# Output projection weights split ahead of time on GpSimd and parked in HBM

## The chip, the core and the metric

The kernel runs on one core of a Trainium2 chip. The metric is the device time of one execution in microseconds (us); the time before is the median of three runs, 1128.26 us (1127.38 to 1130.19). Engines are named as in the profile: PE is TensorE (matmuls), DVE is VectorE, ACT is ScalarE, POOL is GpSimd, SP is SyncE, which issues every DMA of this kernel from one queue, in order.

## The reference, cut to what matters

One layer on 1024 tokens of width 1024. The input projection feeds a pooling group and a gated DeltaNet group; their outputs are joined into `mix`, which goes through the output projection `w_out` (1024 x 1024), and a squared-ReLU MLP follows.

```python
u = rms_norm(h, norm_mix[l])
proj = u @ w_in[l]
pool_out = pool_mixer(proj[..., :P], w_pool[l], pool_scale[l])
qkv = causal_conv_silu(proj[..., P:P + 3 * G], conv_w[l])
...
mix = jnp.concatenate([pool_out, gdn_out], axis=-1)
h = h + mix @ w_out[l]
u = rms_norm(h, norm_mlp[l])
h = h + jnp.square(jax.nn.relu(u @ w_up[l])) @ w_down[l]
return rms_norm(h, norm_final)
```

## The kernel before

Every large product is made of three matmuls in the reduced type fp32r. Each operand is split into a high part (a cast to fp32r, on ACT) and a low part (the operand less its high part, a subtraction), and the product is high x high + high x low + low x high. `split_w` (L128 to L137) does this for a weight: a DMA brings 256 KB into a tile `raw`, ACT casts it into `wh` (L135), and an engine that the caller names subtracts (L136).

The 1024 tokens are taken in two halves of 512. The input projection (`project`, L477) runs for the first half over the columns k, q, v, z, p and then for the second half over k, q, v, p, z. Each letter is two blocks of 256 columns; a block is 48 matmuls of 512 columns on PE and reads four pairs of weight tiles, which live in two rings of five buffers (`wh` and `wl`). In the first half the weights are split and both parts are stored to HBM (`keep_parts`); in the second half `load_parts` (L224) brings the parts back with two DMAs of 256 KB for each pair, so that nothing is split there.

Between these dense matmuls PE runs the chunks of the gated DeltaNet as "strands": generators that are stepped by a clock of the program's own. The order of PE is written out by this clock, and no scheduler moves it. ACT, DVE, POOL and SP are put in order by a scheduler, which estimates when operands arrive. Each engine then runs its list strictly in order, so an instruction that waits holds up all that stand behind it. The strands need ACT and DVE within a few microseconds (`invert` L611: products `pt`, `ptt`, casts `t` and `tt` on ACT at L634 and L635, masks `xx` on DVE at L628; `scan` L672: `y` on ACT at L686). The gate values of the second half (`gates`, L357) are made on ACT and DVE at L366 to L410, two loads of activation tables among them.

After the z columns of the second half comes the output projection (`out_proj2` L813, `out_proj` L803). `wout_weights(n, ks)` (L784) makes the weights of output column half n for the eight row groups k: it loads 256 KB of `w_out` into `raw` (ring of three), casts on ACT and subtracts on DVE. The groups k below 4 go into the `wh`/`wl` rings, k from 4 on into `woh`/`wol`, four buffers each, in the room that the input projection's operands `u` give up at its end (`close(upc)`, L869). For n = 0 both parts are also stored to HBM (`wdo`, L872), because tokens 512 to 1023 need them again later (L929). Tokens 0 to 511 are projected for n = 0 and n = 1, two tiles of 128 tokens at a time; the last chunks of the DeltaNet run in between as strands. The up projection follows and takes its first weights through the same `raw` ring (L1017).

## Time and profile before

| | |
|---|---|
| median of the runs | 1128.26 us |
| the profiled execution, its own time | 1130.39 us |
| its span, first to last instruction | 1128.2 us |
| TensorE clock granted, mean | 0.993 |
| first half of the input projection and its loads | about 0 to 171 us |
| second half of the input projection | about 171 to 365 us |
| output projection, both token halves | about 365 to 485 us |
| HBM read and written | 133.77 MB and 58.72 MB |

Lines of the profile read like this. A group has line, engine, operation, output<-input, how often (x), and the shortest, median and longest duration in ns with the first and last start in us; in the list of waits the columns are who waited for whom, the total in us, how many times, and the longest. A line of the timeline has start and duration in us, engine, line and operation, and in brackets the idle time of the engine just before it and what released it. `SPq` is the issue of a DMA on SP; "to landing" is the time from this issue to the arrival of its last byte.

### The profile page before, as it was taken

Reading aid. Unit: us, or ns where it says so; the run is one execution under the profiler, and the core shown is the slowest. Engines: PE = TensorE matmul, PEld = TensorE weight load, DVE = VectorE, ACT = ScalarE, POOL = GpSimd, SP = SyncE. Lnnn points to the kernel's source line nnn. Section 1 sums busy time; section 2 is a strip of 40 time slices with the busy share of each in tenths; the row PEclk is TensorE's granted clock in tenths of the full one; section 3 lists DMA queues with packets and bytes.
Section 4 is the critical chain, followed back from the end, with each engine's and each line's share of the span. In section 5 each row is a group of like instructions: output and inputs, shape, how many; then the busy total and the mean of one; then the engine's idle time right before and its main releaser. Section 6 shows DMA issues by size and latency. Waiting matters only on the chain.

```text
span 1128.2 us, 15738 instructions
## 1 busy us (share of the span) xinstructions
PE 1091.0 (97%) x5638; PEld 891.5 (79%) x5638; DVE 726.2 (64%) x1212; ACT 573.5 (51%) x1063; POOL 221.6 (20%) x217
## 2 busy tenths in 40 slices
PE   8999999999999999997899999999999999999997
PEld 6787778778888788885678888888888878888886
DVE  5787587757676864556665656565555786476584
ACT  6577566465555553555445545454543333334363
POOL 6122032020220310156333222222000000000020
PEclk9999999999999999998999999999999999999999
DMA  7877643233435620410644444444597995355662
GB/s 241 290 259 263 197 136 98 87 105 115 142 118 195 200 83 31 139 59 12 231 150 149 159 150 159 149 145 163 186 369 252 325 350 186 112 187 192 199 206 75
DMA packets 109975, 193.51 MB, mean 172 GB/s; under 512 B 10373, under 2 KB 39114, under 8 KB 109898
## 3 DMA queue, kind: packets, MB, share of 16 engines
q1 hardware_dynamic: 109898, 192.52, 50.1%
q8 instruction: 44, 0.72, 0.3%
q14 instruction: 33, 0.27, 0.1%
HBM read 133.77 MB, written 58.72 MB: 171 GB/s over the span
## 4 chain that ended last, share of the span: by engine, by line
PE 77%; ACT 4%; DVE 3%; DMA 2%; POOL 2%; issue 1%; POOLq 0%; SPq 0%; DVEq 0%; ACTq 0%
PE bank L44 55%; PE acc L44 21%; DMA x<-hd 1%; PE bank L48 1%; DVE cy L429 1%; DMA raw<-in_w_out_dram 1%; DMA wu<-in_w_up_dram 1%; POOL r L993 0%; POOL wl L1006 0%; ACT rl L554 0%; ACT wh L1005 0%; POOL rk L155 0%; POOL wu L1032 0%; DVE h L1236 0%; DVE xx L628 0%
## 5 line engine op out<-in xcount | busy, mean ns | idle before, releaser
L44 PE MATMUL bank<-th,wh 128*128 128x512 f32 x448 | 177.2, 396 | 9.9 <-DVE u L1090 6.1
L44 PE MATMUL bank<-th,wl 128*128 128x512 f32 x448 | 176.9, 395 | 2.7 <-DVE wl L1006 1.4
L44 PE MATMUL bank<-tl,wh 128*128 128x512 f32 x448 | 176.4, 394 | 0.0
L44 PE MATMUL acc<-uh,wh 128*128 128x512 f32 x320 | 129.5, 405 | 5.7 <-ACT cy L427 2.3
L44 PE MATMUL bank<-th,sh 128*128 128x512 f32 x344 | 133.8, 389 | 0.0
L44 PE MATMUL bank<-th,sl 128*128 128x512 f32 x344 | 133.8, 389 | 0.0
L44 PE MATMUL bank<-tl,sh 128*128 128x512 f32 x344 | 133.8, 389 | 0.0
L1005 ACT CAST wh<-wu 128x512 fp32r<-128x512 f32 x110 | 67.4, 620 | 122.2 <-PE bank L44 100.8
L44 PE MATMUL acc<-ul,wh 128*128 128x512 f32 x320 | 129.4, 404 | 0.0
L44 PE MATMUL acc<-uh,wl 128*128 128x512 f32 x320 | 128.7, 402 | 0.0
L1005 ACT CAST sh<-x 128x1024 fp32r<-128x1024 f32 x55 | 57.9, 1053 | 137.2 <-PE bank L44 137.1
L1006 DVE TENSOR_TENSOR sl<-x,sh 128x1024 fp32r<-128x1024 f32 x55 | 67.2, 1222 | 70.1 <-ACT sh L1005 70.1
L44 PEld LDWEIGHTS bank<-th,wh 128*128 128x128 f32 x448 | 85.0, 190 | 30.9 <-issue 7.0
L44 PEld LDWEIGHTS bank<-th,wl 128*128 128x128 f32 x448 | 84.9, 189 | 22.8 <-DVE wl L1006 2.3
L44 PEld LDWEIGHTS bank<-tl,wh 128*128 128x128 f32 x448 | 85.1, 190 | 18.4
L1006 DVE TENSOR_TENSOR wl<-wu,wh 128x512 fp32r<-128x512 f32 x98 | 74.5, 764 | 34.6 <-ACT wh L1005 33.9
L44 PEld LDWEIGHTS acc<-uh,wh 128*128 128x128 f32 x320 | 60.5, 189 | 19.2 <-ACT cy L427 4.2
L44 PEld LDWEIGHTS bank<-th,sl 128*128 128x128 f32 x344 | 64.6, 188 | 13.6
L44 PEld LDWEIGHTS bank<-th,sh 128*128 128x128 f32 x344 | 64.6, 188 | 13.4
L44 PEld LDWEIGHTS bank<-tl,sh 128*128 128x128 f32 x344 | 64.5, 188 | 13.3
L155 POOL TENSOR_TENSOR stf<-stf,mhalf 128x1 f32<-128x1 f32 x8 | 7.9, 997 | 321.3 <-DVE stf L1255 321.3
L44 PEld LDWEIGHTS acc<-uh,wl 128*128 128x128 f32 x320 | 60.6, 189 | 11.0 <-POOL wl L136 0.3
(321 smaller groups left out, 2191.6 us busy)
## 6 DMA issues: line engine op xcount, KB each, us to landing
w<-in_w_down_dram SPq DMA_DIRECT2D x55, 512.0 KB, 5.5
x<-hd SPq DMA_DIRECT2D x55, 512.0 KB, 3.3
wu<-in_w_up_dram SPq DMA_DIRECT2D x16, 1024.0 KB, 6.0
hd<-s SPq DMA_DIRECT2D x48, 256.0 KB, 2.0
raw<-in_w_in_dram SPq DMA_DIRECT2D x40, 256.0 KB, 4.1
w<-in_w_down_dram SPq DMA_DIRECT2D x32, 256.0 KB, 6.9
xin<-in_x_dram SPq DMA_DIRECT2D x8, 512.0 KB, 5.5
raw<-in_w_out_dram SPq DMA_DIRECT2D x16, 256.0 KB, 4.1
```

The lines of the kernel that those rows point to most:

```text
L44: T0.matmul(out, lhsT, rhs, start=start, stop=stop, skip_group_check=goes_on)
L48: T0.transpose(out, in_, identity)
L155: last["rsqrt"] = G.tensor_tensor(s, s, mhalf[:, :n], op=ALU.pow)
L429: V.scalar_tensor_tensor(cy, cr[:, e:e + HALF], tap[e], cy, op0=ALU.mult, op1=ALU.add)
L1005: A.copy(hi, src)
L1006: eng.tensor_tensor(lo, src, hi.bitcast(F32), op=ALU.subtract)
```

## The change

`wout_weights` no longer splits. All sixteen pieces of `w_out` (n = 0 and 1, k = 0 to 7; piece 0 to 7 and 8 to 15 below) are split by a new function, `split_wout`, which is called at three places in the second half of the input projection. Each piece takes all three buffers of the ring `raw`: the loaded weight, its high part (ACT), its low part (POOL). Both parts are stored to HBM. `wout_weights` then loads both parts with two DMAs for each piece into the same tiles that it filled before. The stores of n = 0 at the start of the output projection are gone, since all parts are in HBM.

```diff
-    def load_parts(kept, pool=None):
+    def load_parts(kept, pool=None, tags=("wh", "wl"), bufs=5):
...
-        return [split_w(wov[:, k, n * HALF:(n + 1) * HALF], [P, HALF], V,
-                        *((pools["wo"], "woh", "wol", 4) if k >= 4 else ())) for k in ks]
+        return [load_parts(wo_parts[n, k], *((pools["wo"], ("woh", "wol"), 4) if k >= 4 else ())) for k in ks]
+
+    def split_wout(n, ks):
+
+        for k in ks:
+            raw, hi, lo = (ws.tile([P, HALF], dt, name="raw", tag="raw", bufs=3) for dt in (F32, F32R, F32R))
+            nc.sync.dma_start(out=raw, in_=wov[:, k, n * HALF:(n + 1) * HALF])
+            A.copy(hi, raw)
+            G.tensor_tensor(lo, raw, hi.bitcast(F32), op=ALU.subtract)
+            wo_parts[n, k] = keep_parts(f"wdo{n}{k}", [(hi, lo)])[0]
...
         yield from project(1, "q", G)
+        split_wout(0, range(KT))
         yield from project(1, "v", G)
+        split_wout(1, range(4))
         yield from project(1, "p", G)
+        split_wout(1, range(4, KT))
         yield from project(1, "z", G, conv_done)
...
-        wo_parts.extend(keep_parts("wdo", wt[0]))
```

The order of PE is the same in both kernels. On the other engines the scheduler puts the new work earlier than the calls stand in the code: the first piece is loaded where the first `w_out` load stood before, and the last is stored among the loads of the second half's first v block.

The first place is the queue of SP around the second block of the q columns (`wd768_` are its weights). Before, only these loads stand there:

```order
L228 DMA wh_3032<-wd768_0h_737 128x512
L228 DMA wl_3034<-wd768_0l_738 128x512
L228 DMA wh_3036<-wd768_1h_741 128x512
L228 DMA wl_3038<-wd768_1l_742 128x512
L228 DMA wh_3040<-wd768_2h_745 128x512
```

In the change, the stores of piece 10 (`wdo120`), pieces 11 and 12 (`wdo130`, `wdo140`) stand among them:

```order
L228 DMA wl_3034<-wd768_0l_738 128x512
L220 DMA wdo120h_3732<-raw_3727 128x512
L220 DMA wdo120l_3733<-raw_3728 128x512
L792 DMA raw_3736<-in_w_out_dram 128x512
L220 DMA wdo130h_3742<-raw_3737 128x512
L220 DMA wdo130l_3743<-raw_3738 128x512
L792 DMA raw_4229<-in_w_out_dram 128x512
L220 DMA wdo140h_4235<-raw_4230 128x512
L220 DMA wdo140l_4236<-raw_4231 128x512
L228 DMA wh_3036<-wd768_1h_741 128x512
L228 DMA wl_3038<-wd768_1l_742 128x512
```

A store waits for ACT or POOL, and the load of the next piece stands behind the store of the low part; the weights `wd768_1` stand behind two whole pieces.

The second place is ACT where the gates of the second half are made (`ge`, table load, then on to `y`). Before:

```order
L430 ACTIVATE kT_2188<-cy_2675 128x512
L666 ACTIVATE v_2764<-bank_2753 128x512
L372 COPY ab2_2778<-bank_2773 128x64
L383 ACTIVATE ge_2784<-gs_2786 128x16
L634 CAST t_2840<-bank_2830 128x512
L389 ACT_TABLE_LOAD
```

In the change, the casts of pieces 11 and 12 stand in the same stretch:

```order
L430 ACTIVATE kT_2188<-cy_2675 128x512
L793 CAST raw_3737<-raw_3736 128x512
L666 ACTIVATE v_2764<-bank_2753 128x512
L372 COPY ab2_2778<-bank_2773 128x64
L383 ACTIVATE ge_2784<-gs_2786 128x16
L793 CAST raw_4230<-raw_4229 128x512
L634 CAST t_2840<-bank_2830 128x512
L389 ACT_TABLE_LOAD
```

Only the two casts are new; each waits for the load of its piece, and `t` and the table load stand behind the second.

The third place is DVE at the start of the output projection, between the masks `xx` of two levels of an inversion. Before, three subtractions of weights stand among them:

```order
L136 TENSOR_TENSOR wol<-raw,woh 128x512
L628 TENSOR_TENSOR xx<-bank,lev_321 128x512
L800 TENSOR_TENSOR ml<-qT,mh 128x512
L136 TENSOR_TENSOR wol<-raw,woh 128x512
L568 TENSOR_SCALAR rk<-rk 128x4
L571 TENSOR_TENSOR kn<-bank,rk 128x512
L136 TENSOR_TENSOR wl<-raw,wh 128x512
L628 TENSOR_TENSOR xx<-bank,lev_329 128x512
```

In the change (`ml` is now L808):

```order
L808 TENSOR_TENSOR ml<-qT,mh 128x512
L628 TENSOR_TENSOR xx<-bank,lev_321 128x512
L568 TENSOR_SCALAR rk<-rk 128x4
L571 TENSOR_TENSOR kn<-bank,rk 128x512
L628 TENSOR_TENSOR xx<-bank,lev_329 128x512
```

The subtractions are gone, and `ml` stands ahead of the first `xx`.

## The prediction

> **What bounds the kernel now.** I read the page first:

> ```profile
> span 1128.2 us, 15738 instructions
> PE 1091.0 (97%) x5638; PEld 891.5 (79%) x5638; DVE 726.2 (64%) x1212; ACT 573.5 (51%) x1063; POOL 221.6 (20%) x217
> ```

> PE is busy for 97% of the span, and its list does not change. An engine that is never idle cannot be fed better: the change can win only idle time of PE, and lose by making more of it. So the next view is the list of waits of PE in the stretch that the removed work fills, 345 to 460 us:

> ```profile
> PE bank L44 <- DVE xx L628: 2.0, 2, 1.4
> PE acc L44 <- ACT r L924: 0.6, 1, 0.6
> ```

> This is all there is to win: 2.0 us in two waits for `xx` (the 0.6 us for `r` belong to the turning of the normalised tokens, which the change does not touch). The timeline of DVE tells what made `xx` late:

> ```profile
> 370.76 1.77 DVE L136 TENSOR_TENSOR wol<-raw,woh 128x512 fp32r<-128x512 f32 x1
> 372.45 0.68 DVE L628 TENSOR_TENSOR xx<-bank,lev 128x512 f16<-128x512 f32 x1
> ...
> 374.13 1.77 DVE L136 TENSOR_TENSOR wol<-raw,woh 128x512 fp32r<-128x512 f32 x1
> ...
> 379.39 0.68 DVE L628 TENSOR_TENSOR xx<-bank,lev 128x512 f16<-128x512 f32 x1
> ```

> Both times subtractions of weights stand ahead of it. The second time the last of them waits for a cast that waits for its load, as the timeline of ACT shows:

> ```profile
> 377.54 0.62 ACT L135 CAST wh<-raw 128x512 fp32r<-128x512 f32 x1 [2.71 <-DMA raw<-in_w_out_dram]
> ```

> The work goes to about 140 to 245 us: by their neighbours in the new order, the pieces lie there. The sum of the windows there, and the waits of PE from 140 to 250 us:

> ```profile
> sum 105.00, PE 100.72 PEld 81.69 DVE 76.81 ACT 63.61 POOL 22.99; mean PE 9.16 PEld 7.43 DVE 6.98 ACT 5.78 POOL 2.09
> ```

> ```profile
> PE bank L44 <- ACT y L686: 1.8, 1, 1.8
> PE bank L44 <- DVE xx L628: 0.9, 1, 0.9
> PE bank L44 <- DVE pl L467: 0.9, 1, 0.9
> ```

> PE is as full here, and where it waits, it waits for ACT and DVE. POOL and ACT have room on average (23.0 and 63.6 of 105 us), so what counts is not the amount of added work but whether a waiting instruction holds up what stands behind it.

> **What goes.** Sixteen subtractions on DVE, sixteen casts on ACT and sixteen stores leave the stretch from 345 to 405 us. Both waits for `xx` lose their cause. What is late next is `xx`'s own matmul, just before it on PE, so I take both waits as gone: -2.0 us. From both sides: nothing is won if `xx` stays late behind `kn`; more than 2.0 us cannot be won, as PE has no other idle time there.

> **What the loads cost.** Each weight tile now comes by DMA alone. The late ones are those of k = 4 to 7, whose room comes free with the last matmul of the input projection, right at the first product of the output projection:

> ```profile
> 365.21 0.40 PE L44 MATMUL acc<-wh,mh 128*128 128x512 f32 x1
> 365.45 0.39 PE L44 MATMUL acc<-wl,mh 128*128 128x512 f32 x1
> ...
> 370.39 0.39 PE L44 MATMUL acc<-woh,mh 128*128 128x512 f32 x1
> ```

> PE first needs `woh` 5.2 us later. The load of k = 4 is second in the queue then. The nearest row for a load of this kind in a stretch with other loads is:

> ```profile
> wl<-wd_0l SPq DMA_DIRECT2D x3, 256.0 KB, 3.1
> ```

> With 0.4 us of issue for each DMA ahead, its two parts land some 3.5 to 4 us after the room is free, before 370.39. Each further piece is 0.8 us of issue later and is needed at least six products of 0.23 us (365.21 to 365.45), 1.4 us, later. So the loads hide behind the products of k = 0 to 3; without that cover the price would be about 4 us, once. For n = 1 the room of each k comes free 24 products (5.5 us) or more ahead of its need, which also covers a landing of 3.1 us. I take 0.

> **What the sixteen pieces cost.** A piece is a chain: load, cast, subtraction on POOL, store of the low part, and only then the load of the next piece, since a piece takes all three buffers. The rows are those of the same tile in its other uses (count, shortest/median/longest in ns):

> ```profile
> L135 ACT CAST wh<-raw x48: 603/621/669, 9.6 to 391.1; 128x512 fp32r<-128x512 f32 x48
> ...
> L131 SPq DMA_DIRECT2D raw<-in_w_out_dram x16: 327/350/732, 138.7 to 399.0; - x16
> L136 POOL TENSOR_TENSOR wl<-raw,wh x8: 1277/1503/1829, 11.2 to 32.1; 128x512 fp32r<-128x512 f32 x8
> ...
> DMA to landing us min/median/max: 2.5/4.1/7.2
> ```

> Cast 0.62, subtraction 1.50, issue of the store 0.35 and a landing make a period. The landing is 2.5 at best, 4.1 in the median, which comes from crowded stretches; I take 2.9, next to the 3.1 of the row above, since the middle stretch moves little else. So a period is 5.4 us, between 5.0 and 6.6. The amounts (16 x 0.62 = 9.9 us on ACT, 16 x 1.50 = 24 us on POOL) fit into the idle time. The stalls don't have to. Where ACT has to run the casts of pieces 3 and 5 without holding anything up is read from its timeline, by the neighbours that the new order gives them:

> ```profile
> 171.11 0.59 ACT L441 COPY pr<-acc 128x512 f32<-128x512 f32 x1 [0.17 <-PE acc L44]
> ...
> 181.71 0.59 ACT L705 COPY on<-bank 128x512 f32<-128x512 f32 x1 [3.54 <-PE bank L44]
> ```

> Piece 3 goes just ahead of `pr` (170.95), and piece 5 ahead of `on`, so it must start by 181.71 - 0.62 = 181.1. Two periods from 170.95 end at 181.7: 0.6 us late, and 0 to 3.0 us over the range. Behind it wait the cast for `pl`, on which PE already waits 0.9 us, and `t`. I count all of it: +0.6.

> The tighter place is where the gates are made:

> ```profile
> 215.60 0.62 ACT L430 ACTIVATE kT<-cy 128x512 f32<-128x512 f32 x1
> ...
> 219.88 0.22 ACT L383 ACTIVATE ge<-gs 128x16 f32<-128x16 f32 x1 [1.26 <-DVE gs L382]
> 221.35 0.59 ACT L634 CAST t<-bank 128x512 f16<-128x512 f32 x1 [1.25 <-PE bank L44]
> 221.95 1.28 ACT L389 ACT_TABLE_LOAD   x1
> ...
> 228.64 0.56 ACT L686 COPY y<-bank 128x512 f32<-128x512 f32 x1
> ```

> Piece 11 is cast after `kT` (216.2), piece 12 between `ge` and `t`, so by 220.7. One period from 216.2 is 221.6: 0.9 us late (0.5 to 2.1). From `t` to `y` ACT works nearly without a gap, and `y` is what PE waits 1.8 us for, so that nothing hides this: +0.9.

> On SP the pieces stand between the weight loads of the input projection. The one behind two whole pieces is this:

> ```profile
> 223.45 0.32 SPq L228 DMA_DIRECT2D wh<-wd_1h  x1
> ...
> 236.26 0.32 SPq L228 DMA_DIRECT2D wh<-wd_3h  x1
> ```

> It goes out once piece 12 is stored, near 221.6 + 0.62 + 1.50 + 0.35 = 224.1 instead of 223.45. The second row waits for a buffer that PE reads until six products before the next block starts, so the block that needs the first row starts after 236. Ten microseconds of cover; I take 0. The other weight loads have a similar lead.

> Last, POOL beside DVE. Where DVE reads two operands from SBUF, one execution can take much longer than the median:

> ```profile
> L429 DVE SCALAR_TENSOR_TENSOR cy<-cr,cols,cy x72: 735/750/1715, 26.9 to 293.9; 128x512 f32<-128x512 f32 x72
> ```

> That is up to 0.97 us more. If half of the sixteen subtractions meet such an operation, at half of that, DVE loses 3.9 us; it has 28 us idle in 105, so I let a fifth of it reach PE: +0.8, between 0 and the 15.5 us of sixteen full blocks. [...]

> **The sum.** -2.0 + 0.6 + 0.9 + 0.8 = +0.3 us. The profiled execution took 1130.39 us, 2.2 us more than its span, so one like it would take 1130.7; it lies 2.1 us above the median of 1128.26. Against the median I predict 1128.6 us. About 0.3%, 3.4 us, is what a measurement of this kernel can tell from no change.

> [...]

> **The rivals.**

> *The chain sets the pace of ACT* (slower). From piece 3 at 170.95 nine periods must end by 220.7, 5.5 us each. At 4.1 us of landing they end at 230.1: PE is 9.4 us late, and with -2.0 and +0.8 the time is 1136.5. It decides once the lateness passes 4.6 us, at a period of 6.0 or a landing of 3.6. For it: the median of 4.1. Against it: the 3.1 of loads in this very stretch. 0.22.

> *DVE falls behind POOL* (slower). [...] 0.08.

> *The gain does not come* (no change): `xx` stays late behind `kn`, and the sum is +2.3, 1130.6. 0.10.

> *The waits from 140 to 250 us shrink too* (faster): the scheduler's new order puts `pl` and the conv steps elsewhere. If the chain costs nothing and half of the 3.6 us quoted goes, -2.0 - 1.8 = -3.8, 1124.5. For it: `pl` stands earlier in DVE's new order. Against: the `y` wait is a dense run on ACT. 0.12.

> **How the numbers follow.** The forecast has 0.48. Faster is the last rival, 0.12; within 0.3% are the forecast and the third, 0.58; slower the first two, 0.30. The range goes down to -3.0 us (1125.3), which leaves out about half of the faster rival, and up to the second rival's 1134.0, which leaves out some 0.13 of the first: about 2 in 10 together.

> **What would show it.** Right: no wait for `xx` near 373 and 380 us; the casts of pieces 5 and 12 held up by their load, by less than 1 us; the wait for `y` grown from 1.8 to about 2.7 us; landings near 2.9 us; no wait for `woh`. Wrong: landings of 3.6 us or more and ACT idle on loads in nearly every piece, waits of PE for DVE that sum to over 8 us before 250 us, a wait of PE for a weight tile, or PE idle less from 140 to 250 us than before.

## The result and the profile after

The changed kernel takes 1134.65 us (median of 6 runs, 1132.0 to 1135.79), the kernel before 1129.02 us beside it (6 runs): a ratio of 1.0052, 95% interval 1.0038 to 1.0066, or 5.9 us more (4.3 to 7.5). The forecast of 1128.6 us was wrong, and the time lies just above its range. The profiled execution took 1135.48 us. Its page begins:

```profile
span 1133.8 us, 15827 instructions
PE 1095.3 (97%) x5638; PEld 894.0 (79%) x5638; DVE 719.0 (63%) x1196; ACT 573.2 (51%) x1063; POOL 244.9 (22%) x233
```

PE does the same 5638 multiplications in the same order, so every instruction of PE can be held against itself. From 345 to 465 us the list of PE's waits is down to one row:

```profile
PE acc L44 <- ACT r L934: 0.6, 1, 0.6
```

Both waits for `xx` are gone, and there is none for `woh`: the gain came. What was lost, was lost earlier. At 139 us PE is 0.1 us late against before, by 246 us it is 8.1 us late, and from 386 us on, behind the two waits that are gone, 5.9 us. PE's waits from 139 to 345 us, after:

```profile
PE bank L48 <- DVE kn L571: 2.3, 2, 1.3
PE bank L44 <- ACT y L686: 2.0, 1, 2.0
PE bank L48 <- DVE wgh L462: 1.6, 1, 1.6
PE bank L44 <- DVE pl L467: 1.6, 2, 1.1
PE bank L44 <- DVE g_hi L394: 0.9, 1, 0.9
PE bank L44 <- DVE xx L628: 0.5, 1, 0.5
PE bank L44 <- ACT t L634: 0.3, 1, 0.3
```

Before, the same list had the three rows that the prediction quotes and these two:

```profile
PE bank L48 <- DVE kn L571: 0.8, 1, 0.8
PE bank L48 <- DVE wgh L462: 0.6, 1, 0.6
```

The sums are 9.2 us after and 5.0 us before: 4.2 us more, not 8.0. The rest is no wait at all. PE's timeline after the two waits near 203 us shows it:

```profile
202.84 0.63 PE L48 MATMUL bank<-ident,kn 128*128 128x128 f32 x4 [1.33 <-DVE kn L571]
204.01 0.38 PE L44 MATMUL bank<-xx,tt 128*128 128x128 f16 x4 [0.54 <-DVE xx L628]
...
205.52 0.63 PE L44 MATMUL acc<-uh,wl 128*128 128x512 f32 x1
205.94 0.63 PE L44 MATMUL acc<-uh,wh 128*128 128x512 f32 x1
```

The last two start 0.42 us apart instead of 0.23. The windows of 1 us there, whose column after the five busy times is the granted clock of PE:

```profile
204.00:205.00 1.00, 0.99 (x9) 0.98 (x9) 0.87 (x2) 1.00 (x4) 1.00 (x2) 0.67 0.78 279
205.00:206.00 1.00, 1.00 (x4) 0.71 (x3) 0.00 (x0) 0.50 (x2) 1.00 (x1) 0.50 0.02 4
206.00:207.00 1.00, 1.00 (x4) 0.81 (x3) 0.00 (x0) 0.00 (x0) 0.01 (x1) 0.50 0.18 63
207.00:208.00 1.00, 1.00 (x4) 0.76 (x4) 0.00 (x0) 0.00 (x0) 0.00 (x0) 0.62 0.79 272
```

Half clock, from 204.3 to 207.8 us: 0.33 + 0.50 + 0.50 + 0.38 = 1.7 us of full-speed work lost. The same happens from 235.1 to 238.5 us, behind the waits for `g_hi` and `y`. Before, the clock was full from 123 to 521 us. So the 8.0 us are 4.2 us of waits, 3.4 us of half clock, and 0.4 us in gaps that the list does not show. The half clock is not the profiled run's alone: the mean granted clock was 0.987 to 0.989 in the six runs of the changed kernel, and 0.992 on average over the runs of the kernel before.

Two things made those waits. One is DVE beside GpSimd's subtractions (L794); all engines near 173 us:

```profile
172.64 0.62 ACT L793 CAST raw<-raw 128x512 fp32r<-128x512 f32 x1 [0.62 <-DMA raw<-in_w_out_dram]
...
173.33 1.28 POOL L794 TENSOR_TENSOR raw<-raw 128x512 fp32r<-128x512 f32 x1 [5.94 <-ACT raw L793]
...
173.53 1.11 DVE L455 TENSOR_TENSOR pr<-hd,pr 128x16 f32<-128x16 f32 x1
...
174.64 0.69 DVE L448 TENSOR_TENSOR nxt<-pr 128x527 f32<-128x527 f32 x1
```

and the operation of L455 in the kernel before:

```profile
170.88 0.17 DVE L455 TENSOR_TENSOR pr<-hd,pr 128x16 f32<-128x16 f32 x1
```

An operation of 0.17 us ends 0.94 us late, as soon as the subtraction does, and what stands behind it on DVE starts late with it. Nine of the sixteen subtractions hold up an operation of DVE; summed over them it loses 7.4 us against the median of the same operations. The other is ACT, where a cast waits for its load, here ahead of the gates:

```profile
215.68 0.62 ACT L793 CAST raw<-raw 128x512 fp32r<-128x512 f32 x1 [2.13 <-DMA raw<-in_w_out_dram]
...
227.34 0.62 ACT L793 CAST raw<-raw 128x512 fp32r<-128x512 f32 x1 [1.86 <-DMA raw<-in_w_out_dram]
227.87 0.58 ACT L634 CAST t<-bank 128x512 f16<-128x512 f32 x1
...
234.88 0.56 ACT L686 COPY y<-bank 128x512 f32<-128x512 f32 x1
```

`y` is 6.2 us later than before, but PE itself was already 4.7 us late there. PE's wait for `y` grew by 0.2 us, and 0.9 us for `g_hi` is new. Not every cast that waits costs PE time: behind those of pieces 5, 9 and 10, which waited 3.3, 4.9 and 2.1 us, PE's list has no wait that is new or longer. Over all pieces ACT waits this long for their loads (us, times), and the loads land after:

```profile
DMA raw<-in_w_out_dram: 15.6, 7
```

```profile
DMA to landing us min/median/max: 2.5/3.1/3.9
```

### The profile page after: what moved, and what is told of

Same layout as the page of the kernel before. It is cut to its first block, busy times and chain, and to the rows that moved or that the text cites. A ratio compares the mean times of both kernels' runs of the same rounds, so it can differ in the third digit from the quotient of the medians.

```text
span 1133.8 us, 15827 instructions
## 1 busy us (share of the span) xinstructions
PE 1095.3 (97%) x5638; PEld 894.0 (79%) x5638; DVE 719.0 (63%) x1196; ACT 573.2 (51%) x1063; POOL 244.9 (22%) x233
## 4 chain that ended last, share of the span: by engine, by line
PE 78%; DVE 3%; ACT 3%; DMA 3%; POOL 2%; issue 1%; SPq 0%; POOLq 0%; ACTq 0%; DVEq 0%
PE bank L44 54%; PE acc L44 22%; DMA raw<-in_w_out_dram 2%; PE bank L48 1%; DMA wu<-in_w_up_dram 1%; DVE cy L429 1%; DMA w<-in_w_down_dram 1%; POOL r L1003 0%; POOL wl L1016 0%; ACT wh L1015 0%; POOL wu L1042 0%; POOL raw L794 0%; DVE h L1246 0%; ACT raw L793 0%; ACT junk L1261 0%
## 5 line engine op out<-in xcount | busy, mean ns | idle before, releaser
L44 PE MATMUL bank<-th,wh 128*128 128x512 f32 x448 | 177.3, 396 | 9.5 <-DVE u L1100 6.1
L44 PE MATMUL bank<-th,wl 128*128 128x512 f32 x448 | 177.0, 395 | 2.6 <-DVE wl L1016 1.4
L44 PE MATMUL bank<-tl,wh 128*128 128x512 f32 x448 | 176.7, 394 | 0.0
L44 PE MATMUL acc<-uh,wh 128*128 128x512 f32 x320 | 130.5, 408 | 5.2 <-DVE zT L503 1.8
L44 PE MATMUL bank<-th,sh 128*128 128x512 f32 x344 | 134.0, 390 | 0.3 <-DVE h L1246 0.3
L44 PE MATMUL bank<-th,sl 128*128 128x512 f32 x344 | 133.9, 389 | 0.0
L44 PE MATMUL bank<-tl,sh 128*128 128x512 f32 x344 | 133.8, 389 | 0.0
L44 PE MATMUL acc<-ul,wh 128*128 128x512 f32 x320 | 130.1, 407 | 0.0
L44 PE MATMUL acc<-uh,wl 128*128 128x512 f32 x320 | 129.1, 403 | 0.0
L44 PEld LDWEIGHTS bank<-th,wh 128*128 128x128 f32 x448 | 85.1, 190 | 30.6 <-issue 7.0
L44 PEld LDWEIGHTS bank<-th,wl 128*128 128x128 f32 x448 | 84.9, 190 | 22.9 <-DVE wl L1016 2.4
L44 PEld LDWEIGHTS bank<-tl,wh 128*128 128x128 f32 x448 | 85.1, 190 | 18.5
L44 PEld LDWEIGHTS bank<-th,sh 128*128 128x128 f32 x344 | 64.6, 188 | 14.5 <-issue 0.7
L44 PEld LDWEIGHTS acc<-uh,wh 128*128 128x128 f32 x320 | 60.9, 190 | 18.7 <-ACT cy L427 3.5
L44 PEld LDWEIGHTS bank<-tl,sh 128*128 128x128 f32 x344 | 64.6, 188 | 13.4
L44 PEld LDWEIGHTS bank<-th,sl 128*128 128x128 f32 x344 | 64.6, 188 | 13.4
L44 PEld LDWEIGHTS acc<-uh,wl 128*128 128x128 f32 x320 | 61.0, 191 | 11.3 <-POOL wl L136 0.2
## 6 DMA issues: line engine op xcount, KB each, us to landing
hd<-s SPq DMA_DIRECT2D x48, 256.0 KB, 2.0
raw<-in_w_in_dram SPq DMA_DIRECT2D x40, 256.0 KB, 4.0
w<-in_w_down_dram SPq DMA_DIRECT2D x32, 256.0 KB, 6.7
raw<-in_w_out_dram SPq DMA_DIRECT2D x16, 256.0 KB, 3.1
```

The source lines that it names most:

```text
L44: T0.matmul(out, lhsT, rhs, start=start, stop=stop, skip_group_check=goes_on)
```

## The experiments

Theory A: the chain on ACT. A cast stands in ACT's queue and waits for a load that goes out only when the piece before it is stored. Theory B: the subtractions on GpSimd, which hold up DVE and what stands behind them on GpSimd. Diffs are against the changed kernel unless it says otherwise; differences in us are the ratio's, times 1129.

**The gain alone.** Fifteen pieces left out:

```
         for k in ks:
+            if wo_parts:
+                wo_parts[n, k] = wo_parts[0, 0]
+                continue
```

> The changed kernel with fifteen of the sixteen pieces left out: only the first is split and stored, and every product of the output projection loads that piece's two parts from HBM. What is left is the gain alone. If the loads of both parts cost nothing: the two waits for xx near 373 and 380 us gone, 1126 to 1127.5 us. If the gain does not come or the loads eat it: 1128 us or more.

Measured: 0.9995 (0.9987 to 1.0004), -0.6 us (1129.06 us), in the range of the second case but for neither of its reasons. The waits for `xx` are gone and there is none for weights, but its one piece makes the wait for `wgh` 1.6 us instead of 0.6, as in the changed kernel. So this is the gain less one piece.

Then the transfers without casts and subtractions:

```
-            A.copy(hi, raw)
-            G.tensor_tensor(lo, raw, hi.bitcast(F32), op=ALU.subtract)
-            wo_parts[n, k] = keep_parts(f"wdo{n}{k}", [(hi, lo)])[0]
+            wo_parts[n, k] = keep_parts(f"wdo{n}{k}", [(h0, h0)])[0]
```

> The changed kernel with the sixteen casts and the sixteen subtractions left out and all transfers kept: each raw piece is loaded and not used, and one tile that is not it is stored twice in its place. If the traffic and SP's queue are part of the loss: 1130 us or more. If not, only the gain is left: 1126 to 1128.5 us.

Measured: 1.0127 (1.0114 to 1.0141), +14.3 us, for another reason than the question: with nothing to wait for, the scheduler put the 32 stores between 20 and 57 us, and by 70 us PE is 10 us late. The sixteen loads ran from 150 to 175 us. It says little on the middle stretch, so the transfers were held there:

```
+            with tc.issue_after(last["parts"].ins):
                 nc.sync.dma_start(out=raw, in_=wov[:, k, n * HALF:(n + 1) * HALF])
                 wo_parts[n, k] = keep_parts(f"wdo{n}{k}", [(h0, h0)])[0]
+            yield 5.5
```

> As the kernel with transfers alone (raw pieces loaded and not used, one other tile stored twice for each), but each group of transfers queued on SP behind the weight loads of its time, so that it lies between about 140 and 300 us and not in the first 70 us, where the kernel with transfers alone lost its time. If the transfers as such cost: 1130 us or more. If they are hidden there: only the gain is left, 1126.5 to 1129 us.

Measured: 1127.43 us beside 1130.09, 0.9978 (0.9966 to 0.9990), -2.5 us. PE's list from 139 to 345 us is that of the kernel before, 5.0 us. The gain is real, and 48 transfers in the middle stretch cost nothing that can be measured. PE waits once for a weight here, 0.26 us for `woh` at 372 us.

**Part by part.** Without the subtractions:

```
-            G.tensor_tensor(lo, raw, hi.bitcast(F32), op=ALU.subtract)
-            wo_parts[n, k] = keep_parts(f"wdo{n}{k}", [(hi, lo)])[0]
+            wo_parts[n, k] = keep_parts(f"wdo{n}{k}", [(hi, hi)])[0]
```

> The changed kernel with the sixteen subtractions left out: the rounded part is stored twice, so load, cast and the two stores stay, and GpSimd has nothing to do with the pieces. Theory B (GpSimd's subtractions hold up DVE's operations, so that wgh, pl and kn come late): the three losses near 156, 178 and 203 us go, with the half clock behind the third, some 5 us, and the wait for y stays: 1129 to 1131 us. Theory A (casts on ACT wait for loads): the chain is only 1.3 us shorter per piece, ACT still waits for most loads, 1132 to 1136 us.

Measured: 1.0032 (1.0021 to 1.0043), +3.6 us. The number (1132.73 us) lies in A's range, at its lower end; the trace has something of both. The waits near 156 and 203 us are those of before, as B has it; but ACT waits 15.7 us for loads, as long as with the subtractions, and this takes its place, with half clock behind it, as A has it:

```profile
PE bank L44 <- ACT ph L466: 2.0, 1, 2.0
```

The same with work on GpSimd that reads nothing:

```
             A.copy(hi, raw)
+            for _ in range(3):
+                G.memset(raw, 0.0)
```

> The kernel without subtractions (the rounded part stored twice, 3.6 us above the kernel before), with three fills of the raw piece on GpSimd behind each cast, so that GpSimd has about as much work at the same places as with a subtraction, but reads nothing from SBUF. If the subtractions cost by keeping DVE from SBUF while GpSimd reads it: DVE's short operations keep their 0.2 us and the time stays near 1132 to 1134 us. If they cost by standing in GpSimd's queue ahead of rk, so and kd: 1135 us or more.

Measured: 1.0034 (1.0019 to 1.0049), +3.8 us, the same as without. A short copy of DVE beside such fills:

```profile
166.66 1.11 POOL L795 MEMSET raw<- 128x512 f32 x2 [0.71 <-ACT raw L793]
166.84 0.37 DVE L447 COPY nxt<-nxt 128x4 f32<-128x4 f32 x1
166.90 0.70 DVE L448 TENSOR_TENSOR nxt<-nxt 128x524 f32<-128x524 f32 x1
```

0.37 us, where a copy of the same line beside a subtraction took 1.14 (at 152.06 us in the changed kernel; 0.16 in the median there). So 48 fills, 25 us on GpSimd between 141 and 214 us, cost PE nothing that can be measured; they write and read nothing. The operation behind the copy, which reads two operands from SBUF, keeps its 0.70 us (the median of its line in the kernel before).

Without the casts:

```
-            A.copy(hi, raw)
-            G.tensor_tensor(lo, raw, hi.bitcast(F32), op=ALU.subtract)
+            G.tensor_tensor(lo, raw, raw, op=ALU.subtract)
```

> The changed kernel with the sixteen casts left out: GpSimd subtracts the raw piece from itself and the result is stored twice, so that load, subtraction and two stores stay and ACT has nothing to do with the pieces. Theory B (GpSimd): the losses near 156 and 203 us stay, with GpSimd itself now waiting for the loads: 1132 to 1138 us. Theory A (ACT): the wait for y falls back to 1.8 us and the time to 1127 to 1130 us.

Measured: 1.0070 (1.0052 to 1.0087), +7.9 us, B's side. The longest wait of PE is 4.0 us for `xx`, which stands on DVE behind two operations, 0.75 us each in the median, that take 3.05 us beside three of GpSimd's, one of them a subtraction:

```profile
201.62 3.05 DVE L429 SCALAR_TENSOR_TENSOR cy<-cr,cols,cy 128x512 f32<-128x512 f32 x2
204.59 0.68 DVE L431 SCALAR_TENSOR_TENSOR kT<-kT,cy 128x512 f32<-128x512 f32 x1
205.20 0.68 DVE L628 TENSOR_TENSOR xx<-bank,lev 128x512 f16<-128x512 f32 x1
```

**Other engines, other buffers, another place.** Four edits that should have helped one theory or the other:

```
-            G.tensor_tensor(lo, raw, ...)
+            V.tensor_tensor(lo, raw, ...)
```

> The changed kernel with the sixteen subtractions on DVE instead of GpSimd. Theory A: the chain of a piece is 0.5 us shorter and no longer stands behind other work of GpSimd, but ACT still waits for loads that go out one at a time (10 us or more of idle time): 1130 to 1134 us. Theory B: the cause is gone and the added 16 x 0.76 us fit into DVE's idle time: 1127 to 1129 us.

Measured: 1.0098 (1.0085 to 1.0111), +11.1 us; neither. Now DVE's queue waits for casts that wait for loads, with PE's feeders behind it (16.4 us of idle time on DVE ahead of nine subtractions). PE waits 4.2 us for `ph`, which also stands behind a waiting cast on ACT:

```profile
182.89 0.62 ACT L793 CAST raw<-raw 128x512 fp32r<-128x512 f32 x1 [2.94 <-DMA raw<-in_w_out_dram]
...
183.54 0.69 DVE L794 TENSOR_TENSOR raw<-raw 128x512 fp32r<-128x512 f32 x1 [0.98 <-ACT raw L793]
...
187.84 0.62 ACT L793 CAST raw<-raw 128x512 fp32r<-128x512 f32 x1 [0.77 <-DMA raw<-in_w_out_dram]
...
188.67 0.60 ACT L466 CAST ph<-pr 128x512 fp32r<-128x512 f32 x1
```

```
-            A.copy(hi, raw)
+            G.tensor_copy(hi, raw)
```

> The changed kernel with the sixteen casts on GpSimd too, so that ACT has nothing to do with the pieces and nothing of ACT's queue waits for a load. Theory A: the waits of PE for y and kn go back to those of before, no half clock near 204 and 235 us, 1126.5 to 1129.5 us, unless GpSimd's queue now holds up rk and kd instead. Theory B: GpSimd works twice as long beside DVE and waits for loads itself: 1136 us or more.

Measured: 1.0080 (1.0059 to 1.0101), +9.0 us, B's side: waits for `tt` (3.9 us) and `kn` (3.3 us).

```
-            raw, hi, lo = (ws.tile([P, HALF], dt, name="raw", tag="raw", bufs=3) for dt in (F32, F32R, F32R))
+            raw = upp.tile([P, HALF], F32, name="raw", tag="raw2", bufs=2)
+            hi, lo = (ws.tile([P, HALF], F32R, name="raw", tag="raw", bufs=3) for _ in "hl")
```

> The changed kernel with two buffers of their own for the raw pieces, so that a piece's load goes out while the piece before it is still split and stored. Theory A (the chain on ACT: a cast stands in ACT's queue and waits for a load that goes out only when the low part before it is stored; the late ACT makes PE wait, and two of the waits put PE on half clock for 3.4 us, 1.7 us each): the 15.6 us that ACT idles on these loads fall below 4 us, no half clock near 204 and 235 us, the time 1127 to 1129 us. Theory B (the subtractions on GpSimd hold up DVE, and GpSimd's own queue): nothing of that changes, 1133 to 1136 us.

Measured: 1.0130 (1.0115 to 1.0144), +14.7 us. ACT's wait for loads fell to 5.1 us, and A's time did not come. The wait moved to GpSimd, whose subtraction now waits for a store to free its buffer, with `rk` behind it and PE's `kn` (4.5 us) behind that:

```profile
153.39 1.71 POOL L795 TENSOR_TENSOR raw<-raw 128x512 fp32r<-128x512 f32 x1 [1.66 <-DMA wdo020l<-raw]
155.21 1.06 POOL L155 TENSOR_TENSOR rk<-rk,mhalf 128x4 f32<-128x4 f32 x1
```

A as stated, with loads as the one thing waited for, fell here.

```
+            with tc.issue_after(last["parts"].ins):
                 nc.sync.dma_start(out=raw, in_=wov[:, k, n * HALF:(n + 1) * HALF])
...
-        split_wout(0, range(KT))
         yield from project(1, "v", G)
-        split_wout(1, range(4))
+        split_wout(0, range(KT))
         yield from project(1, "p", G)
-        split_wout(1, range(4, KT))
+        split_wout(1, range(KT))
```

> The changed kernel with the pieces later: their loads are queued on SP behind the last weight loads of the v block (eight of them) and of the p block (the other eight), so that they run from about 250 us on, where PE of the kernel before waits for nothing. If it is the place that costs, since 140 to 250 us is where PE is already waiting for ACT and DVE: no or few new waits, the xx waits gone, 1126 to 1129 us. If every piece costs PE the same wherever it stands: 1133 us or more.

Measured: 1.0118 (1.0105 to 1.0131), +13.3 us. Later is not free either when the pieces are queued as densely: from 250 us on, where PE waited for nothing, new waits come for `xx` (3.1 us), `hh` (1.7) and `t`, and once for a weight (2.3 us for `wh` at 383.8 us).

**Spread evenly.** So the queues were given slack: loads 5 us ahead, each later step queued behind work of its own time.

```
+            yield 5.0
+            with tc.issue_after(last["act"].ins):
                 A.copy(hi, raw)
+            yield 0.5
+            with tc.issue_after(last["rsqrt"].ins):
                 G.tensor_tensor(lo, raw, hi.bitcast(F32), op=ALU.subtract)
+            yield 1.5
+            with tc.issue_after(last["parts"].ins):
                 wo_parts[n, k] = keep_parts(f"wdo{n}{k}", [(hi, lo)])[0]
+            yield 0.5
```

> The changed kernel with the same sixteen pieces, engines and buffers, but spread evenly from about 135 to 330 us: each load goes out 5 us and more of PE's time ahead of its cast, and cast, subtraction and stores are queued only behind work of their engine that belongs to that time, so that they find their input ready. [...] If the work itself costs (16 casts, 16 subtractions, 48 transfers beside PE's feeders): 1133 us or more.

> As the evenly spread kernel, with the subtractions on DVE instead of GpSimd. If GpSimd's subtractions hold up DVE by about 1 us wherever they meet it, this one is 1 to 3 us faster than the spread kernel with GpSimd: 1126.5 to 1128.5 us. If that plays no part, DVE's own 16 x 0.76 us make it the same or slower: 1128 to 1132 us.

> The evenly spread kernel with the subtractions left out (the rounded part stored twice), so that sixteen casts on ACT, placed where their loads have landed, and the transfers are what is left. If well-placed casts are hidden: 1126.5 to 1129 us, and the subtractions are the whole price of the spread kernels. If 0.62 us on ACT cost PE time wherever they stand: 1130 to 1133 us.

The last one is the first with the subtraction and its `yield` left out; in the second it is on DVE, behind a step of the convolution. The casts then ran from 177 to 326 us in the last and to 353 us in the first. Measured: with GpSimd 1.0053 (1.0034 to 1.0072), +6.0 us; with DVE 1.0030 (1.0018 to 1.0042), +3.4 us (1132.67 us, just above both of its ranges); without subtractions 0.9981 (0.9969 to 0.9994), -2.1 us. In that last kernel no cast waits for a load, PE's waits from 139 to 345 us are 5.2 us, and the gain is whole. So sixteen well-placed casts and all transfers are hidden. The same work queued as early as possible took +3.6 us, so its placing is worth 5.7 us. That is the waiting and the stretch together, since the casts of that kernel ran from 140 to 211 us; the kernel with dense later pieces shows that a later stretch alone does not help. Subtractions are not hidden even so: 8.1 us on GpSimd, 5.5 us on DVE. These prices are not the operations' alone. On GpSimd five casts still wait for their loads, 3.5 us in all; on DVE one cast waits 2.5 us, and DVE idles 2.2 us ahead of four subtractions whose casts are not done. PE's own waits differ by only 1.9 us between the kernel with subtractions on DVE and the one without (7.1 and 5.2 us). The mean granted clock over the twelve runs of each, 0.9908 and 0.9933, makes some 2.8 us of half clock more.

Is that their place on DVE or their amount? Behind `xx` instead of the convolution, and with the first eight pieces only:

```
-            last["dve"] = V.scalar_tensor_tensor(cy, cr[:, e:e + HALF], ...)
+            V.scalar_tensor_tensor(cy, cr[:, e:e + HALF], ...)
...
-            V.tensor_tensor(xx, px, bc(lev[l]), op=ALU.mult)
+            last["dve"] = V.tensor_tensor(xx, px, bc(lev[l]), op=ALU.mult)
```

```
-        for n, k in [(n, k) for n in range(2) for k in range(KT)]:
+        for n, k in [(0, k) for k in range(KT)]:
```

> The evenly spread kernel with subtractions on DVE, each queued behind a step of the inverse (xx) instead of behind a step of the convolution. Behind xx DVE often waits for PE for some 4 us, so that 0.7 us more hold nothing up. If the price of the spread subtractions (from 1127.6 without them to 1132.7 us with them) is a matter of their place on DVE: 1126.5 to 1130 us. If 16 x 0.7 us of DVE cost PE time wherever they stand: 1132 us or more.

> The same with only the eight pieces of the first half split early; those of the second half are split on loading, as in the kernel before. The waits for xx come from the first half, so the gain of 2 us should stay. If the price goes by the number of subtractions: half of that of the kernel with sixteen. If it is zero there: 1126.5 to 1128.5 us here too.

Measured: 1.0041 (1.0026 to 1.0056), +4.6 us, and 1.0022 (1.0010 to 1.0033), +2.5 us. Another place did not help. Eight cost 4.6 us against the kernel without any, sixteen 6.7 us: fewer may cost less, though the two intervals overlap. In the profiles PE's waits from 139 to 345 us are 7.6 and 8.1 us, row by row nearly the same, so the second eight add only 0.5 us of wait. In both kernels DVE idles for casts that are not done, 5.6 us ahead of three subtractions and 5.8 us ahead of four, first here (the kernel with eight):

```profile
191.53 0.69 DVE L801 TENSOR_TENSOR raw<-raw 128x512 fp32r<-128x512 f32 x1 [3.17 <-ACT raw L798]
```

So how much of the price is the operation (0.7 us each, 11 us for sixteen) and how much is its waiting in the queue is not shown.

**Without moving anything.** Edits of the kernel before: subtractions on GpSimd at their old place, for four pieces and for all sixteen.

```
-        return [split_w(wov[:, k, n * HALF:(n + 1) * HALF], [P, HALF], V,
+        return [split_w(wov[:, k, n * HALF:(n + 1) * HALF], [P, HALF], G if n == 0 and k >= 4 else V,
```

> The kernel before, with nothing moved to HBM: only the four subtractions for k = 4 to 7 of the first half, which stood ahead of xx on DVE near 370 to 376 us, go to GpSimd. If those are what made xx late, the 2.0 us come without the pieces: 1126.5 to 1128 us. [...]

> The kernel before with all sixteen subtractions of the output projection's weights on GpSimd, at their old place from 345 to 405 us. If GpSimd has room there: the same as with four of them, 1126.5 to 1128.5 us. If DVE is held up there as it was between 140 and 250 us, or PE waits for low parts: 1129 to 1134 us.

Measured: 0.9997 (0.9986 to 1.0007) and 1.0001 (0.9990 to 1.0011), no change. The waits for `xx` go, and one for `kn` takes their place, in the kernel with four:

```profile
PE bank L48 <- DVE kn L571: 1.4, 1, 1.4
```

No complete kernel here beats the one before.

**The clock.** In the kernel before, one `y` made late by hand:

```
-        A.copy(y, py)
+        for _ in range(4 if c == 2 else 1):
+            A.copy(y, py)
```

> The kernel before with one copy made late by hand: y of the third chunk (near 228 us) is copied four times over instead of once, about 0.5 us each, so that PE's wait of 1.8 us becomes about 3.4 us. If a wait costs its own length: 1.6 us more, 1129.5 to 1130.5 us. If a wait that fills about half of one of the 3.4 us windows also puts PE on half clock for the window after it: 1.7 us more than that, 1131 to 1132.5 us, and the granted clock falls to 0.50 right behind the wait.

Measured: 1132.38 us beside 1128.98, 1.0029 (1.0017 to 1.0040), +3.3 us, for 1.9 us of wait more (the lists show 1.8 and 3.7; the waits for `xx` near 373 and 380 us, on the other hand, fell from 2.0 to 1.0 us). The clock behind it, in the windows of 1 us:

```profile
229.00:230.00 1.00, 1.00 (x7) 1.00 (x8) 0.00 (x0) 0.00 (x0) 0.00 (x0) 0.68 0.00 0
230.00:231.00 1.00, 1.00 (x6) 1.00 (x6) 0.38 (x2) 0.00 (x0) 0.00 (x0) 0.50 0.00 0
231.00:232.00 1.00, 1.00 (x7) 1.00 (x6) 0.74 (x3) 0.00 (x0) 0.00 (x0) 0.50 0.00 0
232.00:233.00 1.00, 1.00 (x8) 1.00 (x7) 0.00 (x0) 0.59 (x1) 0.00 (x0) 0.61 0.00 0
```

0.32 + 0.50 + 0.50 + 0.39 = 1.7 us. A wait of this kernel can cost more than its length.

The changed kernel and its variants in one table: PE's waits from 139 to 345 us (the sum of the list's rows, from one profile each), and the measured time against the kernel before. The kernel with one piece is left out, and so are those with transfers alone and with later pieces, which lose time outside this stretch too.

| kernel | PE's waits, us | time, us |
|---|---|---|
| before | 5.0 | 0 |
| transfers held, no split | 5.0 | -2.5 |
| spread, no subtraction | 5.2 | -2.1 |
| fills for subtractions | 6.8 | +3.8 |
| spread, DVE | 7.1 | +3.4 |
| no subtraction | 7.3 | +3.6 |
| spread, eight on DVE behind xx | 7.6 | +2.5 |
| spread, DVE behind xx | 8.1 | +4.6 |
| changed kernel | 9.2 | +5.9 |
| no cast | 9.9 | +7.9 |
| spread, GpSimd | 10.2 | +6.0 |
| cast on GpSimd too | 12.3 | +9.0 |
| subtraction on DVE | 13.2 | +11.1 |
| two more buffers | 14.6 | +14.7 |

A straight line through the thirteen variants rises by 1.6 us per us of wait: length plus half clock. The profiles bear this out: what PE loses between the instructions that stand at 139 and 345 us in the kernel before is, in every row, the added waits and half of its time at half clock, to within 1.1 us.

## Why the prediction was wrong

- *The gain, -2.0 us*: right. Both waits went, and the kernels with hidden work show -2.5 and -2.1 us.
- *The loads, 0, and the weight loads on SP, 0*: right. PE waits for no weight in the changed kernel.
- *The period, 5.4 us*: from the cast of piece 3 at 172.64 us to that of piece 12 at 227.34 us nine periods take 54.7 us, 6.1 each. From cast to subtraction they take 0.86 us (0.62 taken), the subtraction 1.46 (1.50 taken), from its end to the issue of the next load 0.47 (0.35 taken), from there to the next cast 3.3 (2.9 taken). So the load was short by most, although its median of 3.1 us is near what was taken: the cast of piece 8 waited for a load until 4.7 us after its issue.
- *The stalls on ACT, +0.6 and +0.9*: seven casts waited for loads, 15.6 us in all, where two were taken. Yet PE's new waits behind them are about what was forecast, 1.1 us for 1.5. The cast of piece 5 waited 3.3 us and cost nothing that PE's list shows; that of piece 12 waited 1.9 us and cost 0.9 us for `g_hi` and 0.2 us for `y`. That the size came out near is luck, as the casts that waited and their lateness were others. What was left out is the half clock behind `y`, 1.7 us.
- *DVE behind GpSimd, +0.8*: this is the step that failed, "it has 28 us idle in 105, so I let a fifth of it reach PE". The shares, half of the subtractions, half of 0.97 us and a fifth, were the author's estimate and no run shows them. DVE lost 7.4 us where 3.9 was taken, and it lost them just ahead of what PE needs: the one piece of the kernel with one piece alone makes PE wait 1.0 us more for `wgh`, more than was taken for all sixteen, and near 203 us `kn` costs 1.3 us that were not there before, with 1.7 us of half clock behind it. Both go when the subtractions are left out, and stay or give way to a longer wait when the casts are. The list of PE's waits that the prediction quotes leaves out the rows `kn` and `wgh`, the two that grew by most. An average of idle time did not tell what another operation costs on an engine that feeds PE.
- *A term that was put at nothing*: half clock, 3.4 of the 8.0 us in the profile. The prediction priced each wait at its own length.
- *The rivals*: the mechanisms of both slower ones show in the trace at once. The first, 1136.5 us, had its point of decision right (a period of 6.0 us) and its reason in part (3.6 us or more in five of the eleven landings that can be read), but PE did not follow ACT's lateness. The second, 1134.0 us, came nearest in time by luck: no run shows the 15.5 us of sixteen full blocks. DVE lost 7.4 us, at nine of the sixteen subtractions, and the half clock, 3.4 us, was left out. The faster one came true for one `pl` (0.9 us before, 0.5 after) and was undone by another (1.1 us at 178 us, where `pl` now stands later on DVE). How much each gave in the changed kernel itself can't be read off exactly, since the parts don't add up: taking out the subtractions leaves +3.6 us, taking out the casts +7.9 us.
- The range failed with the sum: its upper end was the second rival alone, and the two mechanisms were never added.

## What to carry to other kernels

When work is moved beside a full PE, ask of each step which in-order queue it enters and what it waits for there: transfers and casts were free once they were queued where their input was ready (-2.1 us, the whole gain), and cost 5.7 us more when queued as early as possible. Idle time averaged over a stretch does not say that an engine that feeds PE has room: sixteen subtractions, spread out, still cost 5.5 to 6.7 us on DVE and 8.1 us on GpSimd, their own waiting included; beside one of those on GpSimd in the changed kernel, an operation of DVE of 0.17 us ended 0.94 us late. Sum PE's waits by stretches of 3.4 us, not one by one: here 70 of the 81 steps of 3.413 us with 1.6 us and more of idling were followed by a step at half clock, 1.7 us on top.

## What the runs showed of the hardware that was not expected

| idle in one step, us | steps | half clock next |
|---|---|---|
| under 1.0 | 2717 | 0 |
| 1.0 to 1.4 | 45 | 1 |
| 1.4 to 1.6 | 23 | 5 |
| 1.6 to 1.8 | 22 | 13 |
| 1.8 to 2.0 | 19 | 17 |
| 2.0 and more | 40 | 40 |

So half clock came behind most steps with 1.6 us and more (half a step is 1.7 us), and what a wait of about that length cost was a matter of luck: the `y` wait of 1.80 us in the kernel before fell across two steps and cost nothing more, while 1.80 us for `zT` at 117 us fell into one and cost 1.7. Over all its runs here, the kernel before took from 1125.5 us, at a mean granted clock of 0.995, to 1133.6 us, at 0.988; 0.007 of 1129 us are 7.9 us.
